# Seven block products in place of eight for the gate and up products of two FFNs

## The chip, the cores and the metric

The kernel runs on one core of a Trainium2 chip. The metric is the device time of one execution, in microseconds (us); lower is better. The engines run side by side, each through its own queue in order: TensorE (PE in the profile, its weight loads PEld), VectorE (DVE), ScalarE (ACT), GpSimd (POOL) and SyncE (SP), which here issues the loads of the weights. An instruction that waits for another engine's result holds up everything behind it in its own queue.

## The reference

A decoder trunk of two layers on x of 512 tokens by 1024 features, float32. Each layer is half an FFN, a token mixer, half an FFN; a last norm follows.

```python
def rmsnorm(x, g):
    xf = x.astype(jnp.float32)
    r = lax.rsqrt(jnp.mean(xf * xf, axis=-1, keepdims=True) + EPS)
    return (xf * r * g.astype(jnp.float32)).astype(x.dtype)

def swiglu(h, w_gate, w_up, w_down):
    return (jax.nn.silu(h @ w_gate) * (h @ w_up)) @ w_down

def reference(x, ...):
    for layer in range(DEPTH):
        x = x + 0.5 * swiglu(rmsnorm(x, ffn1_norm[layer]), ...)
        h = rmsnorm(x, mix_norm[layer])
        x = x + (parallel_s5_stickbreak(h, ...) if layer % 2 == 0 else short_conv_mixer(h, ...))
        x = x + 0.5 * swiglu(rmsnorm(x, ffn2_norm[layer]), ...)
    return rmsnorm(x, final_norm)
```

The hidden width of an FFN is 2752: 21 blocks of 128 and a tail of 64. There are four FFNs, numbered 0 to 3 in the order in which they run: FFN 0, mixer, FFN 1, FFN 2, short convolution, FFN 3. The change touches FFN 1 and FFN 2.

## The kernel before, in words

x lies transposed in SBUF, features on partitions: eight tiles of 128 features by 512 tokens. A product of float32 numbers is made of three passes of a shorter format (float32r): each operand is cut into a high part (a cast to that format, on ScalarE) and a low part (the rest, a subtraction on VectorE), and TensorE adds high times high, low times high and high times low in PSUM (`mm3`, L245 to L247). So one weight unit of 128 by 1024 is loaded to `raw` by SP (L196), cast to `whi` by ScalarE (L207), subtracted to `wlo` by VectorE (L213), and used by 8 x 3 = 24 matmuls with 512 columns (tokens). There are three buffers each of `raw`, `whi` and `wlo`. A unit is cut two units ahead of its use (`advance`, AHEAD = 2), and the load three units further is issued then.

An FFN goes by thirds of the hidden blocks. In a third, each block f has a gate unit and an up unit (a pair); the products go to PSUM banks `ps_A` (six buffers). VectorE multiplies the gate bank by the norm's factor `rb` (L421), ScalarE takes silu (L423), VectorE multiplies again by `rb` (L424) and by the up bank (L433), ScalarE casts the result to `hhi` (L434) and VectorE makes `hlo` (L435). The tail of gate and up is one unit of both. Then eight down units (one for each block of x) multiply with these, into `ps_mm` (two buffers), and VectorE adds half of it to x (L479). In the last third of an FFN the next norm's inputs are made from x there.

The order on every engine is that of the program text, since this part is under a manual schedule: `drive` walks a list of steps, and a unit's step is `advance` (the cut of a later unit), the unit's own products, and its evacuation (`after`). The mixer in between is ordered by a planner of its own that the change does not touch. The last down stage of the kernel (L533 to L545) works on halves of 256 tokens: it is the only place where the kernel before runs long rows of matmuls with 256 columns.

Of the kernel before, what the change touches and what calls it, by code (L numbers as in the profile page):

```python
# [18 lines left out]
S = 512  # L19
NK = D // 128  # L20
EPS = 1e-6
THIRDS = [list(range(0, 8)), list(range(8, 15)), list(range(15, 22))]
TAIL = 21
RAW_BUFS = 3
W_BUFS = 3
AHEAD = 2
# [21 lines left out]
class Unit:  # L48


    def __init__(self, src, cols, products, after):
        self.src, self.cols, self.products, self.after = src, cols, products, after
        self.own = None


class Task:
# [83 lines left out]
class Trunk:  # L140
# [52 lines left out]
    def load(self, n):  # L193
        u = self.units[n]
        u.raw = self.wp.tile([128, 1024], F32, tag="raw", name="raw", bufs=RAW_BUFS)
        self.nc.sync.dma_start(u.raw[:, : u.cols], u.src)  # L196
        self.loaded = n + 1

    def split_tile(self, u, tag):
# [9 lines left out]
    def cut_lo(self, n, engine=None):  # L209
# [6 lines left out]
    def advance(self):  # L216

        n = self.split
        if n < len(self.units):
            self.cut_hi(n)  # L220
            self.cut_lo(n)
        if n + RAW_BUFS < len(self.units):
            self.load(n + RAW_BUFS)

    def drive(self):

        self.prologue()
        for s in self.steps:
            if isinstance(s, Unit):
                if s.own is None:  # L230
# [171 lines left out]
    def ffn(self, n, nxt):  # L402

        st = self
        gu, dn = self.a["gu"], self.a["dn"]
        first = [True]
        nc = self.nc

        def begin():
            st.take_xg()  # L410
            st.h = {}

        self.steps.append(begin)
# [24 lines left out]

        def evac_tail(keep):
            def run():  # L440
                pg = keep[0]
                t = st.fp.tile([128, S], F32, tag="t", name="t", bufs=2)
                s = st.fp.tile([128, S], F32, tag="s", name="s", bufs=2)
                nc.vector.tensor_tensor(t[0:64], pg[0:64], st.rb[0:64], ALU.mult)
                nc.scalar.activation(s[64:128], t[0:64], AF.Silu)
                nc.vector.tensor_tensor(s[64:128], s[64:128], st.rb[64:128], ALU.mult)
                nc.vector.tensor_tensor(s[64:128], pg[64:128], s[64:128], ALU.mult)
                both = st.fp.tile([128, S], F32R, tag="hhi", name="both", bufs=8)
                hi = st.fp.tile([128, S], F32R, tag="hlo", name="hi2", bufs=8)
                nc.scalar.copy(hi[64:128], s[64:128])  # L450
                nc.scalar.copy(both[0:64], s[64:128])
                nc.vector.tensor_tensor(both[64:128], s[64:128], hi[64:128].bitcast(F32), ALU.subtract)
                nc.scalar.copy(hi[0:64], s[64:128])
                nc.gpsimd.memset(hi[64:128].bitcast(F32), 0.0)
                st.h[TAIL] = (both, hi)
            return run

        def down(dt, third):
            fs = THIRDS[third]
# [23 lines left out]
            c0 = sum(len(THIRDS[i]) for i in range(third)) * 128  # L483
            return Unit(dn[n, dt, :, c0:c0 + nf * 128], nf * 128, products, after)

        for third in range(3):
            for f in sorted(THIRDS[third], key=lambda f: (f != TAIL, f)):
                keep = []
                if f == TAIL:
                    st.steps.append(Unit(gu[n, 2 * f], 1024, st.over_x("A", keep), evac_tail(keep)))  # L490
                    continue
                g, u = evac_gate(keep, f), evac_up(keep, f)
                if f == 0:
                    early, keep0 = [g, u], keep
# [12 lines left out]
                pair = [Unit(gu[n, 2 * f], 1024, st.over_x("A", keep), g), Unit(gu[n, 2 * f + 1], 1024, st.over_x("A", keep), u)]
                if f == 0 and n == st.first_ffn:
                    pair[0].products = lambda u, p=pair, k=keep: st.over_x_two("A", p, [k, k])
                    pair[1].products = lambda u: None  # L510
                st.steps += pair
            if third == 2 and nxt == 6:
                st.steps.insert(-1, st.advance)
                st.steps.append(st.advance)
                st.last_down([down(dt, third) for dt in range(NK)])
                break
            for dt in range(NK):
                st.steps.append(down(dt, third))

    def last_down(self, units):  # L520

# [2 lines left out]

        st, nc = self, self.nc
        v = nc.vector
        fs = THIRDS[2]
# [456 lines left out]
    def mixer(self, nxt):  # L984
# [538 lines left out]
        def run():  # L1523
# [6 lines left out]
            for n in range(st.split, end + AHEAD):  # L1530
# [15 lines left out]
    def prologue(self):  # L1546
# [192 lines left out]
```

## Time and profile before

| | |
|---|---|
| median of 3 runs | 1861.44 us (1861.14 to 1862.04) |
| the profiled execution's own time | 1861.36 us |
| its span, first to last instruction | 1859.6 us |
| matmuls on TensorE | 8486 |
| mean granted clock of TensorE | 0.995 |
| VectorE busy | 1044.9 us |
| ScalarE busy | 627.6 us |

Matmuls are pipelined: a 512-column matmul shows 0.39 us in the profile, and the next begins 0.227 us after it began. So a stretch of matmuls is timed from start to start. The other engines' durations are those of one instruction, and the next may begin slightly before its end. Where an engine stood idle, a row says for how long and which instruction released it.

### The profile page before, as it was taken

Reading aid. Unit: us, or ns where it says so; the run is one execution under the profiler, and the core shown is the slowest. Engines: PE = TensorE matmul, PEld = TensorE weight load, DVE = VectorE, ACT = ScalarE, POOL = GpSimd, SP = SyncE. Lnnn points to the kernel's source line nnn. Section 1 sums busy time; section 2 is a strip of 40 time slices with the busy share of each in tenths; the row PEclk is TensorE's granted clock in tenths of the full one; section 3 lists DMA queues with packets and bytes.
Section 4 is the critical chain, followed back from the end, with each engine's and each line's share of the span. In section 5 each row is a group of like instructions: output and inputs, shape, how many; then the busy total and the mean of one; then the engine's idle time right before and its main releaser. Section 6 shows DMA issues by size and latency. Waiting matters only on the chain.

```text
span 1859.6 us, 21763 instructions
## 1 busy us (share of the span) xinstructions
PE 1837.4 (99%) x8486; PEld 1527.0 (82%) x8486; DVE 1044.9 (56%) x1609; ACT 627.6 (34%) x893; POOL 115.6 (6%) x238
## 2 busy tenths in 40 slices
PE   9999999999989999999999999999999999999998
PEld 8887888888867888888888888888888888888888
DVE  6657778656887553444455434445655554344454
ACT  5313222434885332222243222233322333222233
POOL 0280000100000100000010000000100100000000
PEclk9999999999989999999999999999999999999999
DMA  4334344446411233233332323333322223323231
GB/s 163 116 97 148 113 143 135 136 163 220 125 46 58 83 109 102 91 91 102 95 109 91 102 91 94 99 102 89 105 100 93 91 91 102 102 92 98 97 102 66
DMA packets 77829, 197.71 MB, mean 106 GB/s; under 512 B 20304, under 2 KB 27488, under 8 KB 77728
## 3 DMA queue, kind: packets, MB, share of 16 engines
q1 hardware_dynamic: 77552, 196.30, 33.1%
q8 instruction: 66, 1.08, 0.2%
q14 instruction: 35, 0.29, 0.0%
q10 hardware_dynamic: 144, 0.03, 0.0%
q0 software_dynamic: 32, 0.01, 0.0%
HBM read 180.45 MB, written 12.58 MB: 104 GB/s over the span
## 4 chain that ended last, share of the span: by engine, by line
PE 90%; POOL 3%; DVE 3%; ACT 2%; issue 1%; DMA 1%; DVEq 0%; SPq 0%; POOLq 0%; ACTq 0%
PE ps_A L245 19%; PE ps_A L247 19%; PE ps_A L246 19%; PE ps_mm L245 8%; PE ps_mm L247 8%; PE ps_mm L246 8%; PE ps_mm L1442 1%; PE ps_A L1037 1%; PE ps_A L1039 1%; PE ps_A L1038 1%; PE ps_mm L1443 1%; PE ps_mm L1444 1%; PE ps_mm L1037 0%; DVE wlo L213 0%; PE ps_mm L1038 0%
## 5 line engine op out<-in xcount | busy, mean ns | idle before, releaser
L245 PE MATMUL ps_A<-xhi,whi 128*128 128x512 f32 x1568 | 611.6, 390 | 0.4 <-ACT xhi L297 0.4
L246 PE MATMUL ps_A<-xhi,wlo 128*128 128x512 f32 x1568 | 610.4, 389 | 1.4 <-DVE wlo L213 1.4
L247 PE MATMUL ps_A<-xlo,whi 128*128 128x512 f32 x1568 | 610.3, 389 | 0.1
L213 DVE TENSOR_TENSOR wlo<-raw,whi 128x1024 fp32r<-128x1024 f32 (+1 forms) x324 | 398.7, 1231 | 137.2 <-ACT whi L207 135.9
L207 ACT CAST whi<-raw 128x1024 fp32r<-128x1024 f32 (+1 forms) x324 | 331.9, 1025 | 386.3 <-PE ps_mm L247 228.3
L246 PEld LDWEIGHTS ps_A<-xhi,wlo 128*128 128x128 f32 x1568 | 294.4, 188 | 63.4 <-DVE wlo L213 2.3
L245 PEld LDWEIGHTS ps_A<-xhi,whi 128*128 128x128 f32 x1568 | 294.4, 188 | 62.0 <-issue 0.8
L247 PEld LDWEIGHTS ps_A<-xlo,whi 128*128 128x128 f32 x1568 | 294.3, 188 | 61.8 <-DVE xlo L303 0.5
L245 PE MATMUL ps_mm<-hhi,whi 128*128 128x512 f32 (+1 forms) x672 | 256.6, 382 | 0.0
L246 PE MATMUL ps_mm<-hhi,wlo 128*128 128x512 f32 (+1 forms) x672 | 256.3, 381 | 0.0
L247 PE MATMUL ps_mm<-hlo,whi 128*128 128x512 f32 (+1 forms) x672 | 256.3, 381 | 0.0
L423 ACT ACTIVATE s<-t 128x512 f32<-128x512 f32 x84 | 53.1, 632 | 290.3 <-DVE t L421 290.3
L479 DVE SCALAR_TENSOR_TENSOR x<-ps_mm,x 128x512 f32<-128x512 f32 x88 | 60.8, 691 | 155.8 <-PE ps_mm L247 148.4
L434 ACT CAST hhi<-s 128x512 fp32r<-128x512 f32 x84 | 52.2, 621 | 284.9 <-DVE s L433 284.9
L245 PEld LDWEIGHTS ps_mm<-hhi,whi 128*128 128x128 f32 x672 | 126.3, 188 | 24.5 <-issue 0.4
L247 PEld LDWEIGHTS ps_mm<-hlo,whi 128*128 128x128 f32 x672 | 126.3, 188 | 24.4
L246 PEld LDWEIGHTS ps_mm<-hhi,wlo 128*128 128x128 f32 x672 | 126.3, 188 | 24.3
L421 DVE TENSOR_TENSOR t<-ps_A,rb 128x512 f32<-128x512 f32 x84 | 57.9, 690 | 108.4 <-PE ps_A L247 102.3
L433 DVE TENSOR_TENSOR s<-ps_A,s 128x512 f32<-128x512 f32 x84 | 58.0, 690 | 104.1 <-PE ps_A L247 103.4
L424 DVE TENSOR_TENSOR s<-s,rb 128x512 f32<-128x512 f32 x84 | 58.2, 692 | 63.3 <-ACT s L423 63.3
L435 DVE TENSOR_TENSOR hlo<-s,hhi 128x512 fp32r<-128x512 f32 x84 | 58.2, 693 | 57.7 <-ACT hhi L434 57.7
L297 ACT ACTIVATE xhi<-x,norms 128x512 fp32r<-128x512 f32 x48 | 34.5, 723 | 99.1 <-DVE x L479 60.8
(348 smaller groups left out, 1574.3 us busy)
## 6 DMA issues: line engine op xcount, KB each, us to landing
raw<-gu SPq DMA_DIRECT2D x170, 512.0 KB, 3.3
raw<-dn SPq DMA_DIRECT2D x64, 448.0 KB, 3.3
raw<-dn SPq DMA_DIRECT2D x32, 512.0 KB, 3.5
raw<-sci SPq DMA_DIRECT2D x24, 512.0 KB, 3.3
raw<-ab SPq DMA_DIRECT2D x16, 512.0 KB, 3.3
raw<-abo SPq DMA_DIRECT2D x8, 512.0 KB, 3.3
raw<-sco SPq DMA_DIRECT2D x8, 512.0 KB, 3.3
x<-xT SPq DMA_DIRECT2D x8, 256.0 KB, 5.4
```

What stands on the lines that cost most here:

```text
L207: self.nc.scalar.copy(u.hi[:, : u.cols], u.raw[:, : u.cols])
L213: (engine or self.nc.vector).tensor_tensor(u.lo[:, :c], u.raw[:, :c], u.hi[:, :c].bitcast(F32), ALU.subtract)
L245: nc.tensor.matmul(ps, whi, xhi, start=start and i == 0, stop=False)
L246: nc.tensor.matmul(ps, wlo, xhi, start=False, stop=False)
L247: nc.tensor.matmul(ps, whi, xlo, start=False, stop=stop and i == n - 1)
L421: nc.vector.tensor_tensor(t, pg, st.rb, ALU.mult)
L423: nc.scalar.activation(s, t, AF.Silu)
L424: nc.vector.tensor_tensor(s, s, st.rb, ALU.mult)
L433: nc.vector.tensor_tensor(s, pu, s, ALU.mult)
L434: nc.scalar.copy(hi, s)
L435: nc.vector.tensor_tensor(lo, s, hi.bitcast(F32), ALU.subtract)
L479: nc.vector.scalar_tensor_tensor(x, keep[0], 0.5, x, ALU.mult, ALU.add)
```

## The change

In FFN 1 and FFN 2 the blocks are dealt out anew: the tail goes to the first third (after block 1), and the second and last thirds hold seven full blocks each, so 14 pairs per FFN, 28 in all. For these, gate and up of one block are taken as one 256 by 1024 matrix in two by two parts (gate or up, first or second half of the features), and normalized x as two by two parts (first or second half of the features, first or second half of the tokens). The four parts of the result come from seven block products with sums of the parts in place of eight products of parts. Each of the seven has four k-blocks of 128 and three passes, with 256 columns. The sums of weights (`s12`, `s34`) are made from `raw` on VectorE for every pair and cut to high and low like weights (`shi`, `slo`; the up unit's second half becomes `ahi`, `alo`). x is normalized with `rb` first (`seven_x`), then its sums are made once per FFN, beside the first third's down units (`seven_sums`, `seven_lower`). The results are recombined by adds on VectorE between the products, two of them from banks into which a later product accumulates.

```diff
+PLAIN_THIRDS = [list(range(0, 8)), list(range(8, 15)), list(range(15, 22))]
+SEVEN_THIRDS = [list(range(0, 7)) + [TAIL], list(range(7, 14)), list(range(14, 21))]
+SEVEN = (1, 2)
+THIRDS = [SEVEN_THIRDS if n in SEVEN else PLAIN_THIRDS for n in range(4)]
...
+    def cuts(self, count):
+
+        for _ in range(count):
+            n = self.split
+            if n < len(self.units):
+                if self.units[n].mate is not None:
+                    yield from self.cut_mate(n)
+                    continue
+                self.cut_hi(n)
+                self.cut_lo(n)
+                if self.units[n].paired:
+                    yield
+                    continue
+            self.refill(n)
+            yield
+
+    def cut_mate(self, n):
...
+        nc.scalar.copy(u.q_hi, w[:, b])
+        v.tensor_tensor(s[0][:, a], w[:, a], w[:, b], ALU.add)
+        yield
+        v.tensor_tensor(s[0][:, b], s[0][:, a], g[:, a], ALU.subtract)
+        nc.scalar.copy(u.s_hi[0], s[0])
+        yield
+        v.tensor_tensor(s[1][:, a], g[:, a], w[:, a], ALU.subtract)
+        v.tensor_tensor(s[1][:, b], g[:, b], s[0][:, b], ALU.subtract)
+        nc.scalar.copy(u.s_hi[1], s[1])
+        yield
+        v.tensor_tensor(u.q_lo, w[:, b], u.q_hi.bitcast(F32), ALU.subtract)
+        self.split = n + 1
+        self.refill(n - 1)
+        self.refill(n)
+        yield
+        for i in range(2):
+            v.tensor_tensor(u.s_lo[i], s[i], u.s_hi[i].bitcast(F32), ALU.subtract)
+            yield
...
         for third in range(3):
-            for f in sorted(THIRDS[third], key=lambda f: (f != TAIL, f)):
+            seven = n in SEVEN and third
+            if seven:
+                pairs = [(Unit(gu[n, 2 * f], 1024, None, None), Unit(gu[n, 2 * f + 1], 1024, None, None)) for f in thirds[third]]
+                for f, (g, u) in zip(thirds[third], pairs):
+                    g.paired, u.mate = True, g
+                    st.steps += [[g, u], lambda f=f, u=u: st.seven_products(f, u)]
+                st.steps.append(st.flush)
...
             for dt in range(NK):
-                st.steps.append(down(dt, third))
+                s = down(dt, third)
+                more = n in SEVEN and third < 2
+                if more and dt == 6:
+                    st.steps.append(st.advance)
+                s.split_before = more and dt == 7
+                st.steps.append(s)
+                if more and third == 0:
+                    st.steps += [lambda p=p: p() for p in st.seven_parts(dt)]
...
+    def seven_products(self, f, u):
...
+        cut = self.cuts(2)
+        more = lambda: next(cut, None)
...
+        def product(ps, w, c, b, first):
+
+            for k in range(4):
+                hi, lo = (p[:, c + k * 128:c + k * 128 + 128] for p in w)
+                xhi, xlo = b(k)
+                for n, (a, m) in enumerate(((hi, xhi), (lo, xhi), (hi, xlo))):
+                    nc.tensor.matmul(
+                        ps, a, m, start=first and k == 0 and n == 0, stop=k == 3 and n == 2, skip_group_check=True)
...
+        product(x, gate, 0, b11, True)
+        more()
+        nc.scalar.copy(p1, x)
+        self.flush()
+        y = self.bank("A")[:, l]
+        product(y, s12, 512, t2, True)
+        more()
+        v.tensor_tensor(u1, y, p1, ALU.add)
+        product(x, gate, 512, b21, False)
+        more()
+        nc.scalar.activation(s[:, l], x, AF.Silu)
+        more()
+        product(y, s12, 0, t1, False)
+        more()
+        v.tensor_tensor(u3, y, p1, ALU.add)
+        z = self.bank("A")[:, l]
+        product(z, s34, 0, t3, True)
+        more()
+        v.tensor_tensor(up[:, r], z, u3, ALU.add)
+        product(y, s34, 512, b22, False)
+        more()
+        v.tensor_tensor(s[:, r], y, p1, ALU.add)
+        nc.scalar.activation(s[:, r], s[:, r], AF.Silu)
+        product(z, (u.q_hi, u.q_lo), 0, t4, False)
+        v.tensor_tensor(up[:, l], z, u1, ALU.add)
+        v.tensor_tensor(s, s, up, ALU.mult)
+        hi = self.fp.tile([128, S], F32R, tag="hhi", name="hhi", bufs=8)
+        lo = self.fp.tile([128, S], F32R, tag="hlo", name="hlo", bufs=8)
+        nc.scalar.copy(hi, s)
+        self.h[f] = (hi, lo)
+        self.pending = lambda: v.tensor_tensor(lo, s, hi.bitcast(F32), ALU.subtract)
+        deque(cut, maxlen=0)
```

What this does to the queues is seen in the middle of FFN 1's second third. On VectorE before, one pair of units stands like this (`t` and `s` are the evacuation of the gate, `wlo` the cuts):

```order
L421 TENSOR_TENSOR t<-ps_A,rb 128x512
L424 TENSOR_TENSOR s<-s,rb 128x512
L213 TENSOR_TENSOR wlo<-raw,whi 128x1024
L433 TENSOR_TENSOR s<-ps_A,s 128x512
L435 TENSOR_TENSOR hlo<-s,hhi 128x512
L213 TENSOR_TENSOR wlo<-raw,whi 128x1024
```

And in the changed program, on VectorE, from the last adds of one pair into the next pair (`u` is u1, `alo` the low part of the up unit's second half):

```order
L706 TENSOR_TENSOR s<-ps_A,up 128x256
L709 TENSOR_TENSOR up<-ps_A,u_6857 128x256
L710 TENSOR_TENSOR s<-s,up 128x512
L220 TENSOR_TENSOR wlo<-raw,whi 128x1024
L715 TENSOR_TENSOR hlo<-s,hhi 128x512
L263 TENSOR_TENSOR s_7021<-raw 128x512
L692 TENSOR_TENSOR u_6986<-ps_A,up 128x256
L265 TENSOR_TENSOR s_7021<-s_7021,raw 128x512
L268 TENSOR_TENSOR s_7022<-raw 128x512
L269 TENSOR_TENSOR s_7022<-raw,s_7021 128x512
L272 TENSOR_TENSOR alo<-raw,ahi 128x512
L699 TENSOR_TENSOR s<-ps_A,up 128x256
```

The cut of a later gate unit now stands between the multiply of one pair (L710) and the first add of the next (L692), with `hlo` and a weight sum behind it.

On ScalarE before, in the same place (`s` is silu):

```order
L423 ACTIVATE s<-t 128x512
L207 CAST whi<-raw 128x1024
L434 CAST hhi<-s 128x512
L207 CAST whi<-raw 128x1024
L423 ACTIVATE s<-t 128x512
```

And in the changed program on ScalarE, from the second silu of one pair into the next (`up` is the copy of the first product):

```order
L707 ACTIVATE s<-s 128x256
L713 CAST hhi<-s 128x512
L214 CAST whi<-raw 128x1024
L687 COPY up<-ps_A 128x256
L262 CAST ahi<-raw 128x512
L266 CAST shi<-s_7279 128x1024
L695 ACTIVATE s<-ps_A 128x256
L270 CAST shi<-s_7280 128x1024
```

The gate unit's cast stands behind the cast of the finished pair (L713) as before, and the copy of the next pair's first product (L687) stands behind it.

## Rows read from the trace of the kernel before

**Rows 1.** The page: busy time, and the chain of waits, by engine.

```profile
PE 1837.4 (99%) x8486; PEld 1527.0 (82%) x8486; DVE 1044.9 (56%) x1609; ACT 627.6 (34%) x893; POOL 115.6 (6%) x238
...
PE 90%; POOL 3%; DVE 3%; ACT 2%; issue 1%; DMA 1%; DVEq 0%; SPq 0%; POOLq 0%; ACTq 0%
```

**Rows 2.** FFN 1 by stretch: busy PE, PEld, DVE, ACT, POOL; clock, DMA.

```profile
698.50:742.00 43.50, 43.50 (x193) 36.02 (x193) 16.02 (x17) 8.96 (x9) 0.00 (x0) 1.00 0.33 101
...
742.00:818.00 76.00, 76.00 (x337) 62.92 (x336) 35.57 (x41) 21.31 (x27) 0.00 (x0) 1.00 0.29 92
```

**Rows 3.** Matmuls in order of time (start, duration, engine, line).

```profile
1772.64 0.39 PE L245 MATMUL ps_A<-xhi,whi 128*128 128x512 f32 x1
...
1775.36 0.39 PE L245 MATMUL ps_A<-xhi,whi 128*128 128x512 f32 x1
...
1812.83 0.28 PE L245 MATMUL ps_A<-hhi,whi 128*128 128x256 f32 x1
...
1814.27 0.28 PE L245 MATMUL ps_A<-hhi,whi 128*128 128x256 f32 x1
```

**Rows 4.** Weight loads by line and shape: busy, mean ns.

```profile
L246 PEld LDWEIGHTS ps_A<-hhi,wlo 128*128 128x128 f32 x48 | 9.2, 192 | 0.0
```

**Rows 5.** A hand-over from TensorE to VectorE, in order of time.

```profile
1835.20 0.28 PE L545 MATMUL ps_mm<-hi,wlo 128*128 128x256 f32 x1
...
1835.52 0.42 DVE L550 SCALAR_TENSOR_TENSOR x<-ps_mm,x 128x256 f32<-128x256 f32 x1 [0.57 <-PE ps_mm L545]
```

**Rows 6.** VectorE operations by line and shape: busy, mean ns, idle before.

```profile
L435 DVE TENSOR_TENSOR hlo<-s,hhi 128x512 fp32r<-128x512 f32 x84 | 58.2, 693 | 57.7 <-ACT hhi L434 57.7
...
L550 DVE SCALAR_TENSOR_TENSOR x<-ps_mm,x 128x256 f32<-128x256 f32 x8 | 3.4, 424 | 4.3 <-PE ps_mm L545 4.3
```

**Rows 7.** VectorE and ScalarE in order of time; a pair in FFN 1.

```profile
776.05 0.69 DVE L433 TENSOR_TENSOR s<-ps_A,s 128x512 f32<-128x512 f32 x1 [1.82 <-PE ps_A L247]
...
776.78 0.62 ACT L434 CAST hhi<-s 128x512 fp32r<-128x512 f32 x1 [3.80 <-DVE s L433]
...
777.30 1.05 ACT L207 CAST whi<-raw 128x1024 fp32r<-128x1024 f32 x1
...
778.38 1.23 DVE L213 TENSOR_TENSOR wlo<-raw,whi 128x1024 fp32r<-128x1024 f32 x1 [0.26 <-ACT whi L207]
```

**Rows 8.** VectorE operations that follow one another, in order of time.

```profile
331.99 0.69 DVE L424 TENSOR_TENSOR s<-s,rb 128x512 f32<-128x512 f32 x1 [0.76 <-ACT s L423]
...
332.60 0.68 DVE L928 TENSOR_TENSOR qt<-qsi 128x512 f32<-128x512 f32 x1
...
399.57 1.22 DVE L213 TENSOR_TENSOR wlo<-raw,whi 128x1024 fp32r<-128x1024 f32 x1 [0.81 <-ACT whi L207]
...
400.71 0.68 DVE L1226 SCALAR_TENSOR_TENSOR qk<-ps_A,rb 128x512 f32<-128x512 f32 x1
...
1222.01 1.23 DVE L213 TENSOR_TENSOR wlo<-raw,whi 128x1024 fp32r<-128x1024 f32 x1 [1.55 <-ACT whi L207]
...
1223.26 0.69 DVE L421 TENSOR_TENSOR t<-ps_A,rb 128x512 f32<-128x512 f32 x1
...
1288.94 1.09 DVE L213 TENSOR_TENSOR wlo<-raw,whi 128x896 fp32r<-128x896 f32 x1 [0.60 <-ACT whi L207]
```

**Rows 9.** The page: loads of gate and up, KB, us to landing.

```profile
raw<-gu SPq DMA_DIRECT2D x170, 512.0 KB, 3.3
```

**Rows 10.** TensorE's gaps in the mixer, and its granted clock by stretch.

```profile
520.55 0.33 PE L1373 MATMUL ps_mm<-wh,v 128*128 128x128 f32 x1 [1.79 <-ACT sig L1467]
...
535.68 0.33 PE L1340 MATMUL ps_A<-sph,mk_neg 128*128 128x128 f32 x1 [1.11 <-DVE sp L1314]
...
538.90 0.47 PE L1340 MATMUL ps_A<-sph,mk_tri 128*128 128x128 f32 x1 [1.46 <-DVE sp L1314]
...
521.00:528.00 7.00, 6.03 (x18) 0.51 0.19 69
...
539.00:540.00 1.00, 1.00 (x5) 0.50 0.00 0
```

More of the change, by code (lines that the diff above doesn't have):

```diff
@@ L52, in __init__ @@
         self.src, self.cols, self.products, self.after = src, cols, products, after
-        self.own = None
+        self.own = self.mate = None
+        self.paired = self.split_before = False
 class Task:
@@ L195, in load @@
         u.raw = self.wp.tile([128, 1024], F32, tag="raw", name="raw", bufs=RAW_BUFS)
-        self.nc.sync.dma_start(u.raw[:, : u.cols], u.src)
+        at = 0
+        for src in u.src if isinstance(u.src, list) else [u.src]:
+            self.nc.sync.dma_start(u.raw[:, at:at + src.shape[-1]], src)
+            at += src.shape[-1]
         self.loaded = n + 1
@@ L214, in cut_lo, with refill, advance @@
         self.split = n + 1
[L216 to L221, printed above, removed]
+    def refill(self, n):
         if n + RAW_BUFS < len(self.units):
             self.load(n + RAW_BUFS)
+    def advance(self):
+        deque(self.cuts(1), maxlen=0)
+    def cuts(self, count):
[13 more added lines that the diff above has]
+    def cut_mate(self, n):
+        nc, sp = self.nc, self.sp7
+        v = nc.vector
+        u = self.units[n]
+        g, w = u.mate.raw, u.raw
+        a, b = slice(0, 512), slice(512, 1024)
+        u.q_hi = sp.tile([128, 512], F32R, tag="ahi", name="ahi", bufs=2)
+        u.q_lo = sp.tile([128, 512], F32R, tag="alo", name="alo", bufs=2)
+        s = [sp.tile([128, 1024], F32, tag="s12", name="s12"), sp.tile([128, 1024], F32, tag="s34", name="s34")]
+        u.s_hi = [sp.tile([128, 1024], F32R, tag="shi", name="shi", bufs=3) for _ in range(2)]
+        u.s_lo = [sp.tile([128, 1024], F32R, tag="slo", name="slo", bufs=3) for _ in range(2)]
+        nc.scalar.copy(u.q_hi, w[:, b])
[16 more added lines that the diff above has]
+            yield
     def drive(self):
@@ L229, in drive @@
             if isinstance(s, Unit):
-                if s.own is None:
+                if s.own is None and not s.split_before:
                     self.advance()
@@ L407, in ffn @@
         nc = self.nc
+        thirds = THIRDS[n]
         def begin():
@@ L411, in begin @@
             st.h = {}
+            if n == SEVEN[0]:
+                st.open("sp7")
         self.steps.append(begin)
@@ L458, in down @@
         def down(dt, third):
-            fs = THIRDS[third]
+            fs = thirds[third]
             nf = len(fs)
@@ L481, in after @@
                     st.feed_norm(nxt, dt)
-            c0 = sum(len(THIRDS[i]) for i in range(third)) * 128
-            return Unit(dn[n, dt, :, c0:c0 + nf * 128], nf * 128, products, after)
+            src = [dn[n, dt, :, fs[0] * 128:(fs[-1] + 1) * 128]]
+            if fs[-1] - fs[0] != nf - 1:
+                src = [dn[n, dt, :, fs[0] * 128:(fs[-2] + 1) * 128], dn[n, dt, :, TAIL * 128:(TAIL + 1) * 128]]
+            return Unit(src, nf * 128, products, after)
         for third in range(3):
-            for f in sorted(THIRDS[third], key=lambda f: (f != TAIL, f)):
+            seven = n in SEVEN and third
[5 more added lines that the diff above has]
+                st.steps.append(st.flush)
+            for f in [] if seven else sorted(thirds[third], key=lambda f: (f != TAIL or third == 0, f if f != TAIL else 1.5)):
                 keep = []
@@ L511, in ffn @@
                 st.steps += pair
+                if n in SEVEN and 3 <= f < 7:
+                    st.steps.append(lambda i=f - 3: st.seven_x(n, i))
             if third == 2 and nxt == 6:
@@ L517, in ffn @@
             for dt in range(NK):
-                st.steps.append(down(dt, third))
+                s = down(dt, third)
[6 more added lines that the diff above has]
+                    st.steps += [lambda p=p: p() for p in st.seven_parts(dt)]
+        if n == SEVEN[-1]:
+            st.steps.append(lambda: st.open_pools.pop().__exit__(None, None, None))
@@ new lines, in seven_x @@
+    def seven_x(self, n, i):
+        tag = ("s12", "s34", "slo", "slo")[i]
+        if i == 0:
+            self.xn, self.b7, self.t7, self.pending = {}, {}, {}, None
+        self.xn[i] = self.sp7.tile([128, 1024], F32, tag=tag, name="xn", bufs=3 if tag == "slo" else 1)
+        for j in range(2):
+            k = i + 4 * j
+            self.nc.vector.scalar_tensor_tensor(
+                self.xn[i][:, j * 512:(j + 1) * 512], self.x[k], self.norms[:, (0, 2, 3, 5)[n], k:k + 1], self.rb, ALU.mult, ALU.mult)
@@ new lines, in seven_parts, with seven_sums @@
+    def seven_parts(self, dt):
+        i = {0: 0, 1: 1, 3: 2, 5: 3}.get(dt)
+        j = {1: 0, 2: 1, 4: 2, 6: 3}.get(dt)
+        return [lambda: self.seven_sums(i)] * (i is not None) + [lambda: self.seven_lower(j)] * (j is not None)
+    def seven_sums(self, i):
+        nc, v, x = self.nc, self.nc.vector, self.xn[i]
+        b11, b12, b21, b22 = (x[:, c:c + 256] for c in range(0, 1024, 256))
+        t = self.fp.tile([128, 512], F32, tag="t", name="t12", bufs=2), self.fp.tile([128, 512], F32, tag="s", name="t34", bufs=2)
+        l, r = slice(0, 256), slice(256, 512)
+        hi = [self.xgp.tile([128, 512], F32R, tag="xhi", name="thi") for _ in range(2)]
+        b = self.sp7.tile([128, 768], F32R, tag="bhi", name="bhi", bufs=4)
+        v.tensor_tensor(t[0][:, l], b12, b11, ALU.subtract)
+        nc.scalar.copy(b[:, 0:256], b11)
+        v.tensor_tensor(t[0][:, r], b22, t[0][:, l], ALU.subtract)
+        nc.scalar.copy(hi[0], t[0])
+        v.tensor_tensor(t[1][:, l], b22, b12, ALU.subtract)
+        v.tensor_tensor(t[1][:, r], b21, t[0][:, r], ALU.subtract)
+        nc.scalar.copy(hi[1], t[1])
+        nc.scalar.copy(b[:, 256:768], x[:, 512:1024])
+        self.t7[i], self.b7[i] = [t, hi], [b]
@@ new lines, in seven_lower @@
+    def seven_lower(self, i):
+        v, x = self.nc.vector, self.xn[i]
+        t, hi = self.t7[i]
+        lo = [self.xgp.tile([128, 512], F32R, tag="xlo", name="tlo") for _ in range(2)]
+        for a, h, o in zip(t, hi, lo):
+            v.tensor_tensor(o, a, h.bitcast(F32), ALU.subtract)
+        b = self.b7[i][0]
+        o = self.sp7.tile([128, 768], F32R, tag="blo", name="blo", bufs=4)
+        v.tensor_tensor(o[:, 0:256], x[:, 0:256], b[:, 0:256].bitcast(F32), ALU.subtract)
+        v.tensor_tensor(o[:, 256:768], x[:, 512:1024], b[:, 256:768].bitcast(F32), ALU.subtract)
+        self.t7[i], self.b7[i] = (hi, lo), (b, o)
@@ new lines, in flush, with part, total @@
+    def flush(self):
+        if self.pending is not None:
+            self.pending()
+        self.pending = None
+    def seven_products(self, f, u):
+        nc, v, g = self.nc, self.nc.vector, u.mate
+        cut = self.cuts(2)
+        more = lambda: next(cut, None)
+        l, r = slice(0, 256), slice(256, 512)
+        def product(ps, w, c, b, first):
[5 more added lines that the diff above has]
+                        ps, a, m, start=first and k == 0 and n == 0, stop=k == 3 and n == 2, skip_group_check=True)
+        def part(j):
+            return lambda k: [p[:, j * 256:j * 256 + 256] for p in self.b7[k]]
+        def total(j):
+            c = slice(j % 2 * 256, j % 2 * 256 + 256)
+            return lambda k: [p[j // 2][:, c] for p in self.t7[k]]
+        b11, b21, b22 = (part(j) for j in range(3))
+        t1, t2, t3, t4 = (total(j) for j in range(4))
+        gate, s12, s34 = (g.hi, g.lo), (u.s_hi[0], u.s_lo[0]), (u.s_hi[1], u.s_lo[1])
+        s = self.fp.tile([128, S], F32, tag="s", name="s", bufs=2)
+        up = self.fp.tile([128, S], F32, tag="t", name="up", bufs=2)
+        p1, u3 = up[:, l], s[:, r]
+        u1 = self.tp.tile([128, S], F32, tag="sq", name="u1", bufs=2)[:, l]
+        x = self.bank("A")[:, l]
+        product(x, gate, 0, b11, True)
[30 more added lines that the diff above has]
+        deque(cut, maxlen=0)
@@ L526, in last_down @@
         v = nc.vector
-        fs = THIRDS[2]
+        fs = THIRDS[3][2]
         out = st.a["out"]
```

1 line of the change is left out of this document (removed).

## The prediction

> **What bounds the kernel now.** I began with the page's busy line and the engine shares of its chain of waits [rows 1]: TensorE is busy 99% of the 1859.6 us span and is 90% of the chain. Next came the busy time by stretch, inside the stretches that the change rewrites [rows 2]. In the second FFN's (FFN 1's) second third, 742 to 818 us, TensorE is busy 76.00 of 76.00 us at granted clock 1.00, VectorE 35.57, ScalarE 21.31. Nothing but the matmul stream sets the time there, so I priced that stream: twelve 512-column matmuls take 1775.36 - 1772.64 = 2.72 us [rows 3], 0.2267 each. A gate and up pair is 2 x 8 x 3 = 48 of them: 10.88 us.
>
> **The change: TensorE's own work.** Seven products of 4 k-blocks x 3 passes are 84 matmuls of 256 columns. The last down stage runs such matmuls, each with its own weights: twelve take 1814.27 - 1812.83 = 1.44 us [rows 3], 0.120 each. The weight loads are busy 192 ns each [rows 4] yet set no pace there. So a pair needs 84 x 0.120 = 10.08 us, 0.80 less; for 28 pairs 22.4 us. Halving the columns saves less than half of a matmul (0.120 against 0.113), so an eighth less arithmetic is 7% less time.
>
> **A page against the row.** The Trainium skill ("TensorE: Matmul & The Clock Gate", Back-to-back issue gap) gives N/2.4 + 2.5 ns per matmul. By it, as an estimate, the pair would fall from 10.36 to 9.17 us and the loop below would be 11.06 against 10.36, slower again by 0.7. The rows above are longer at both sizes; the sum goes by them.
>
> **What the change adds beside TensorE: a loop.** Call the products P1 to P7 in their order in seven_products. P1's result is copied (ScalarE, L687), then P3 accumulates into its bank; P2's bank is read by u1 (L692), then P4 accumulates into it. So P4 may not start until u1 is done; likewise P6 waits for u3 and P7 for the add at L703. Now VectorE is strictly in order, and u1 stands behind: the previous pair's last add (L709, after P7), its multiply (L710), the next pair's wlo (L220), hlo of the previous pair, one weight sum (L263). And wlo waits for whi, which on ScalarE stands behind hhi (L713), which waits for that multiply. This is a ring that closes once per pair: P4, P5, P6, P7, add, multiply, hhi, whi, wlo, hlo, sum, u1, P4. Queued behind the held wlo is all other VectorE work of the pair, and TensorE's queue stops at P4.
>
> Its price, from rows:
> - P4 to P7: 48 x 0.120 = 5.76 us.
> - The end of P7: the last matmul lasts 0.28, 0.16 beyond its place in the stream, and VectorE starts 0.04 later [rows 5]: 0.20.
> - Add at 256 columns from PSUM: 0.42 [rows 6]; 0.03 to the next.
> - Multiply, hhi, whi, up to the start of wlo: the kernel before runs exactly this chain, from the multiply at 776.05 to wlo at 778.38 [rows 7]: 2.33 us (0.69, 0.62 of which whi overlaps the last 0.10, 1.05, hand-overs).
> - wlo, hlo, sum: instructions that need not wait start 0.08 before their predecessor ends. 331.99 to 332.60 is 0.61 for a 0.69 us operation, 399.57 to 400.71 is 1.14 for 1.22 [rows 8]. So 1.15 + 0.61 + 0.61 = 2.37.
> - u1 0.42, and 0.05 to TensorE, an estimate from the hand-overs in rows 5 and 7 (0.03 to 0.04).
>
> From the end of P7 in the stream to P4 that is 0.20 + 0.45 + 2.33 + 2.37 + 0.47 = 5.82 us. TensorE has only P1 to P3 for it, 36 x 0.120 = 4.32: it stands 1.50 us per pair, 0.4 of it ahead of P3 (the copy of P1 stands behind whi) and 1.1 ahead of P4. Period: 5.76 + 5.82 = 11.58 us, against 10.88 before. The kernel before has the same chain with no harm: a cut there is made two units (10.9 us) ahead of its use, and no accumulation waits for VectorE in mid-product.
>
> Is VectorE itself the limit? Its fifteen instructions per pair, back to back, are 3 x 1.15 + 7 x 0.61 + 5 x 0.34 = 9.4 us, plus 1.65 idle while hhi and whi run: 11.1. Close, but the ring is longer.
>
> **Sum over the stretches.** Each of four stretches has seven pairs. The first finds its cuts done in the down units and P4 not late: 10.08 us in the two last thirds. In the two second thirds the eighth down unit has no room: VectorE must in two units of 23 x 0.2267 = 5.21 us do x (0.69), four sums (1.5), wait for ScalarE's casts until 4.6, then wlo, five 512-wide and two 1024-wide operations (6.5), x and the last tlo and blo (2.2): its blo comes some 13.4 us after the start, P1's last block wants it at 11.7. I take 1.7 plus 0.3 at P4: 12.1. In each last pair the sum before u1 is replaced by a second wlo of 896 columns (1.09 against 0.69 [rows 8, 6]) and both wlo are that size: 11.86. The other twenty are 11.58. Total 2 x 10.08 + 2 x 12.1 + 4 x 11.86 + 20 x 11.58 = 323.4, against 28 x 10.88 = 304.6: 18.8 us slower.
>
> **What costs nothing.** The tail block moves from the last third to the first: the same 24 matmuls, and its short down product (two instead of three) goes along. The eight normalizing operations (8 x 0.69 [rows 6]) lie in the first third, the x sums and their parts (some 4.2 us of VectorE for each of four) beside the downs, where VectorE is busy 16.02 of 43.50 us [rows 2]; the last of them is charged above, and without that cover each would cost its length. The 16 extra 64 KB loads of down weights stand on SP's queue, two units before use. Loads of a pair now go out as two in a row after the cut; at 3.3 us to landing each [rows 9], even end to end they have landed 6.6 us after issue, 2 us ahead of the next cut. If that margin fails, whi waits and the ring grows by as much. TensorE's own sequence of banks needs three of six per pair, so none is short.
>
> The profiled run's own time is 1861.36 us (span 1859.6), the median of the runs shown 1861.44; so I add to 1861.4: **1880 us**, 1% slower.
>
> **Rivals.**
> 1. *Instructions on VectorE do not overlap.* With waits on nearly every one of them, each could start after its predecessor's end: 1222.01 to 1223.26 is 1.25 for 1.23 [rows 8]. Then VectorE itself is the limit: 3 x 1.23 + 7 x 0.69 + 5 x 0.42 + 1.75 + 0.2 = 12.5 us per pair, and with the longer first pairs 42 us in all: 1903. Against it, the two other pairs in that group: wlo there had waits too, long met. By a rule of the Trainium skill ("VectorE: DVE Perf Modes", The DRAIN you can't avoid) the next operation starts only when the pipeline is empty, except for one that isn't held; the trace agrees with the exception, mostly. 0.14.
> 2. *The clock falls in the gaps.* In the mixer TensorE stood 1.79 us before 520.55, and the granted clock in 521 to 528 was 0.51, the 1.2 GHz level, for 7 us [rows 10]. My gaps are 1.1 and 0.4 per pair, smaller singly but recurrent, and 1.7 at two places. Seven us at half speed lose 3.5 us of matmul time; a fall within P4 to P7 costs about 3 of them, since that half of the ring is TensorE's own. Three to ten falls: 1889 to 1910; in every pair, 1955. In the mixer again, a gap of 1.11 us before 535.68 left the clock up, and a second of 1.46 before 538.90 brought it to 0.50 in 539 to 540 [rows 10]: two such gaps within 4.3 us are more than mine. 0.19.
> 3. *The ring is hidden, TensorE stays the bound: faster.* This holds if the path from P7 to u1 takes at most 4.32 us; below 5.12 the change breaks even (5.76 + 5.12 = 10.88). Then the time is 1861.4 - 22.4 + 4 for the starts of the second thirds = 1843. For it: TensorE has no wait at all in these stretches today, and VectorE is less than half busy [rows 2]. Against it: 2.33 us of the path is measured as one piece, and nothing in the order of the two queues lets whi pass hhi. 0.08.
> 4. *About no change*, the ring near 10.9 because some of wlo, hlo and the sum is shorter than in these rows: 0.05.
>
> Were the weight loads to set the pace after all (192 ns each), a pair would take 16.1 us and the kernel 146 us more; rows 3 and 4 exclude it.
>
> **How the numbers follow.** My case has 0.54 and its own range is 1872 to 1889 (0.3 us per ring either way). The time is its 1880. The range for 8 in 10 leaves out the faster rival and the clock falling in every pair: 1864 to 1912. A measurement here tells 0.2%, 3.7 us, from no change. Faster: 0.08; same: 0.05; slower: 0.87.
>
> **What would show it.** Right: in the seven-product stretches TensorE waits some 0.4 us before P3 (for L687) and 1.1 us before P4 (for L692), VectorE's longest wait there is wlo for whi, some 1.65 us per pair, and P1 of successive pairs are 11.6 us apart; outside these stretches nothing moves. Matmuls of 256 columns come every 0.120 us. Wrong: no waits of TensorE there and a pair of 10.1 us; or a granted clock under 1.00 in them (rival 2); or VectorE with no idle time and pairs of 12.5 us (rival 1).

## The result, and the profile after

The changed kernel takes 1884.41 us (median of four, 1882.82 to 1886.18) beside 1861.29 us for the kernel before in the same session (median of four): ratio 1.0126, 95% interval 1.0108 to 1.0143. It is slower by 1.3%; 1880 was forecast, inside 1864 to 1912. The profiled execution took 1882.82 us, with a span of 1881.1.

The page of the changed kernel, busy time and the chain by engine, answers to [rows 1]:

```profile
PE 1828.1 (97%) x9494; PEld 1558.1 (83%) x9494; DVE 1204.3 (64%) x1941; ACT 697.9 (37%) x1037; POOL 115.5 (6%) x238
...
PE 80%; DVE 8%; ACT 5%; issue 3%; POOL 3%; DMA 0%; DVEq 0%; SPq 0%; POOLq 0%; ACTq 0%
```

TensorE is busy 9.3 us less than before, so the time did not go into matmuls. Its share of the chain fell from 90% to 80%, and VectorE (3% to 8%) and ScalarE (2% to 5%) took most of what it lost. The stretches of FFN 1 (busy PE, PEld, DVE, ACT, POOL; clock; DMA) say where, in answer to [rows 2]:

```profile
746.00:817.00 71.00, 63.95 (x511) 61.52 (x509) 53.40 (x85) 29.23 (x47) 0.00 (x0) 1.00 0.25 87
865.00:935.00 70.00, 62.95 (x501) 60.52 (x501) 53.17 (x84) 28.46 (x46) 0.00 (x0) 1.00 0.26 86
700.00:734.00 34.00, 34.00 (x152) 28.15 (x151) 25.59 (x43) 16.79 (x25) 0.00 (x0) 1.00 0.29 87
```

In both seven-product stretches TensorE stands idle 7 us of 70, where it had no gap in 76 [rows 2]; in the downs (700 to 734) it still has none. The clock is 1.00 throughout. What it waits for stands in the view of its waits (us in total, times, longest):

```profile
PE ps_A L667 <- DVE u L692: 21.3, 24, 1.1
PE ps_A L667 <- ACT up L687: 6.9, 24, 0.3
...
PE ps_A L302 <- DVE wlo L220: 2.9, 3, 1.4
PE ps_A L667 <- DVE blo L645: 2.9, 2, 1.4
```

Twenty-four of 28 pairs wait for u1 (L692) and for the copy of P1 (L687); the other four are the first of each stretch, whose cuts were made in the downs. The last two rows are smaller waits, below. VectorE's own waits, for the five pairs between 746 and 805 us:

```profile
DVE wlo L220 <- ACT whi L214: 8.2, 5, 1.6
DVE up L709 <- PE ps_A L667: 2.2, 5, 0.4
```

VectorE stands 1.64 us per pair ahead of wlo. One turn of the ring in order of time, from the end of P7 to the next P4:

```profile
781.52 0.28 PE L667 MATMUL ps_A<-tlo,ahi 128*128 128x256 f32 x1
...
781.84 0.42 DVE L709 TENSOR_TENSOR up<-ps_A,u 128x256 f32<-128x256 f32 x1 [0.44 <-PE ps_A L667]
...
782.37 0.69 DVE L710 TENSOR_TENSOR s<-s,up 128x512 f32<-128x512 f32 x1
...
783.09 0.62 ACT L713 CAST hhi<-s 128x512 fp32r<-128x512 f32 x1 [1.25 <-DVE s L710]
...
783.62 1.04 ACT L214 CAST whi<-raw 128x1024 fp32r<-128x1024 f32 x1
...
784.57 0.36 ACT L687 COPY up<-ps_A 128x256 f32<-128x256 f32 x1
784.69 1.22 DVE L220 TENSOR_TENSOR wlo<-raw,whi 128x1024 fp32r<-128x1024 f32 x1 [1.63 <-ACT whi L214]
...
784.98 0.38 PE L667 MATMUL ps_A<-bhi,whi 128*128 128x256 f32 x1 [0.31 <-ACT up L687]
...
785.84 0.68 DVE L715 TENSOR_TENSOR hlo<-s,hhi 128x512 fp32r<-128x512 f32 x1
...
786.44 0.68 DVE L263 TENSOR_TENSOR s<-raw 128x512 f32<-128x512 f32 x1
787.04 0.41 DVE L692 TENSOR_TENSOR u<-ps_A,up 128x256 f32<-128x256 f32 x1
...
787.51 0.39 PE L667 MATMUL ps_A<-thi,shi 128*128 128x256 f32 x1 [0.84 <-DVE u L692]
```

Each line starts when the one that it waits for, for its operand or in its queue, is done: the add, the multiply, hhi, whi, then wlo, with u1 three instructions behind it, and P4 behind u1. TensorE's two rows with a bracket are its two stops of the turn (0.31 before P3, 0.84 before P4). They come to less than the 1.65 us by which the pair is longer than 10.08: a matmul's modelled end (0.28) reaches 0.16 past its place in the stream, and the first matmul after a stop lasts 0.38 to 0.39, 0.1 more. So a stop costs its row and about 0.25. This 0.25 counts as busy in the record; 50 such stops are some 12.5 us, an estimate, and so TensorE's busy time fell by 9.3 us and not by the 22.4 of its shorter work.

From the first matmul of each pair to the next, the pairs of FFN 1's second third take 12.03 us, then 11.73 for the five in the middle, then 11.89; those of its last third 10.07, 11.73 for the five and 11.89; and FFN 2 the same. The 28 pairs take 326.4 us against 304.6.

### The profile page after: what moved, and what is told of

The parts are those of the page before. It is cut to its first block, busy times and chain, and to the rows that moved or that the text cites. A ratio compares the mean times of both kernels' runs of the same rounds, so it can differ in the third digit from the quotient of the medians.

```text
span 1881.1 us, 24317 instructions
## 1 busy us (share of the span) xinstructions
PE 1828.1 (97%) x9494; PEld 1558.1 (83%) x9494; DVE 1204.3 (64%) x1941; ACT 697.9 (37%) x1037; POOL 115.5 (6%) x238
## 4 chain that ended last, share of the span: by engine, by line
PE 80%; DVE 8%; ACT 5%; issue 3%; POOL 3%; DMA 0%; DVEq 0%; SPq 0%; POOLq 0%; ACTq 0%
PE ps_A L302 13%; PE ps_A L301 13%; PE ps_A L303 13%; PE ps_A L667 10%; PE ps_mm L301 7%; PE ps_mm L302 7%; PE ps_mm L303 7%; ACT whi L214 2%; DVE wlo L220 1%; DVE s L710 1%; DVE hlo L715 1%; ACT hhi L713 1%; DVE s L263 1%; PE ps_mm L1640 1%; PE ps_A L1235 1%
## 5 line engine op out<-in xcount | busy, mean ns | idle before, releaser
L302 PE MATMUL ps_A<-xhi,wlo 128*128 128x512 f32 x1120 | 436.4, 390 | 3.0 <-DVE wlo L220 2.9
L301 PE MATMUL ps_A<-xhi,whi 128*128 128x512 f32 x1120 | 437.6, 391 | 0.1
L303 PE MATMUL ps_A<-xlo,whi 128*128 128x512 f32 x1120 | 436.0, 389 | 0.1
L302 PEld LDWEIGHTS ps_A<-xhi,wlo 128*128 128x128 f32 x1120 | 210.3, 188 | 47.8 <-DVE wlo L220 4.4
L301 PEld LDWEIGHTS ps_A<-xhi,whi 128*128 128x128 f32 x1120 | 210.2, 188 | 45.4 <-ACT whi L214 0.9
L303 PEld LDWEIGHTS ps_A<-xlo,whi 128*128 128x128 f32 x1120 | 210.2, 188 | 44.3 <-DVE xlo L359 0.5
L301 PEld LDWEIGHTS ps_mm<-hhi,whi 128*128 128x128 f32 x672 | 126.3, 188 | 24.6 <-issue 0.4
L667 PE MATMUL ps_A<-thi,shi 128*128 128x256 f32 x336 | 97.7, 291 | 21.3 <-DVE u L692 21.3
L667 PE MATMUL ps_A<-thi,slo 128*128 128x256 f32 x336 | 95.0, 283 | 0.0
L667 PE MATMUL ps_A<-tlo,shi 128*128 128x256 f32 x336 | 95.0, 283 | 0.0
L667 PEld LDWEIGHTS ps_A<-thi,shi 128*128 128x128 f32 x336 | 64.3, 191 | 26.6 <-DVE u L692 26.6
```

The source lines that it names most:

```text
L301: nc.tensor.matmul(ps, whi, xhi, start=start and i == 0, stop=False)
L302: nc.tensor.matmul(ps, wlo, xhi, start=False, stop=False)
L303: nc.tensor.matmul(ps, whi, xlo, start=False, stop=stop and i == n - 1)
L667: nc.tensor.matmul(ps, a, m, start=first and k == 0 and n == 0, stop=k == 3 and n == 2, skip_group_check=True)
```

## The experiments

All are edits of the changed kernel; times are medians, ratios stand against the kernel before on the same chip.

**The gate unit's whi ahead of hhi.** The ring has hhi before whi only because the next gate unit is cut after the pair is finished. Here its high part is cast behind P7 and ahead of the add; a few further lines, not shown, keep it from being cast a second time and leave the last pair of a third as it is.

```diff
         product(z, (u.q_hi, u.q_lo), 0, t4, False)
+        deque(cut, maxlen=0)
+        if not last:
+            self.cut_hi(self.split)
+            self.units[self.split].early = True
         v.tensor_tensor(up[:, l], z, u1, ALU.add)
...
-        deque(cut, maxlen=0)
```

> One edit of the changed kernel: on ScalarE the cast of the next gate unit's weights (whi) stands ahead of the finished pair's cast hhi instead of behind it; VectorE's order and its work are the same. Theory (the ring through multiply, hhi, whi, wlo, u1): VectorE no longer stands 1.65 us per pair ahead of wlo, the path from P7 to u1 falls from 5.9 to 4.3 us, as long as P1 to P3, TensorE's waits before P3 and P4 go, a pair is 10.1 us (10.08 by matmuls) and the time 1842 to 1848 us, faster than the kernel before. Rival (VectorE's total work per pair is the limit): a pair stays above 11 us and the time above 1865 us.

Measured: 1846.86 us (1845.44 to 1847.52), ratio 0.9924 [0.9908, 0.9941]; the middle pairs take 10.08 us, the last of each third 10.56. A stretch of it (busy PE, PEld, DVE, ACT, POOL; clock):

```profile
749.00:800.00 51.00, 51.00 (x427) 51.00 (x426) 47.82 (x77) 26.07 (x41) 0.00 (x0) 1.00 0.29 101
```

VectorE and ScalarE there, in order of time (L715 is the multiply, L718 hhi):

```profile
768.86 1.03 ACT L214 CAST whi<-raw 128x1024 fp32r<-128x1024 f32 x1
769.54 0.69 DVE L715 TENSOR_TENSOR s<-s,up 128x512 f32<-128x512 f32 x1
770.15 1.22 DVE L220 TENSOR_TENSOR wlo<-raw,whi 128x1024 fp32r<-128x1024 f32 x1
770.27 0.62 ACT L718 CAST hhi<-s 128x512 fp32r<-128x512 f32 x1 [0.38 <-DVE s L715]
```

TensorE has no gap, with the same instructions as the changed kernel and the same order on VectorE, and wlo follows the multiply after 0.61 us in place of 2.32. So 37.5 us hang on the order of two casts on ScalarE. VectorE's work in full (47.82 of 51.00 us) fits under the products.

**Two subtractions on VectorE left out**, those of the weight sums' low parts; the high parts stand in for them.

```diff
-        u.s_lo = [sp.tile([128, 1024], F32R, tag="slo", name="slo", bufs=3) for _ in range(2)]
+        u.s_lo = u.s_hi
...
-            v.tensor_tensor(u.s_lo[i], s[i], u.s_hi[i].bitcast(F32), ALU.subtract)
```

> One edit of the changed kernel: the two 1024-wide subtractions per pair that make the low parts of the weight sums are left out (the high parts are used in their place, so these two low passes compute something else); 2.3 us less of VectorE per pair, none of it on the path from P7 to u1. Theory (ring): no change, 1881 to 1887 us, TensorE's waits for u1 and for the copy as before. Rival (VectorE's total work is the limit): the pair falls towards TensorE's 10.08 us and the time to 1842 to 1852 us.

Measured: 1880.90 us (1879.82 to 1883.21), ratio 1.0110 [1.0095, 1.0125]. The middle pairs stay at 11.73, and TensorE's waits are those of the changed kernel:

```profile
PE ps_A L666 <- DVE u L691: 21.3, 24, 1.1
PE ps_A L666 <- ACT up L686: 6.9, 24, 0.3
```

VectorE is busy 1145.8 us by the page in place of 1204.3, 2.1 us less per pair, and no turn of the ring got shorter: VectorE's load is not what bounds the pair. The medians are 3.5 us apart, about the spread of these four runs (3.4). In the traces the pairs differ in the first of each second third alone, 10.07 in place of 12.03, where these operations stood ahead of blo: 3.9 us for the two.

**u1 ahead of wlo.** The copy of P1 and u1 are issued before the cut, and hlo after it.

```diff
         product(x, gate, 0, b11, True)
-        more()
         nc.scalar.copy(p1, x)
-        self.flush()
...
         v.tensor_tensor(u1, y, p1, ALU.add)
+        more()
+        self.flush()
+        more()
```

> One edit of the changed kernel: u1 is issued on VectorE ahead of wlo, hlo and the first weight sum of the pair, and the copy of P1 ahead of whi on ScalarE. Theory (an in-order VectorE that is held for 1.65 us per pair, and then meets the next bank into which TensorE accumulates): the wait before P4 goes and comes back at P6, which waits for u3 behind the same work: some 1.6 us per pair there, pair 11.7 us, time 1881 to 1890 us. Rival (u1's place alone is at fault): the waits go, pair 10.1 us, time 1842 to 1848 us.

Measured: 1883.14 us (1882.49 to 1884.03), ratio 1.0120 [1.0105, 1.0136]; the middle pairs take 11.84. Beside the late blo of two first pairs, TensorE's waits in the pairs are down to one:

```profile
PE ps_A L667 <- DVE s L699: 33.0, 24, 1.5
```

The stops at P3 and P4 are gone, and one of 1.48 us stands at P6 of each middle pair, for u3 (L699), longer than the two together (1.15). In order of time:

```profile
786.74 0.42 DVE L689 TENSOR_TENSOR u<-ps_A,up 128x256 f32<-128x256 f32 x1 [1.73 <-PE ps_A L667]
...
787.09 1.22 DVE L220 TENSOR_TENSOR wlo<-raw,whi 128x1024 fp32r<-128x1024 f32 x1
...
792.43 0.39 PE L667 MATMUL ps_A<-bhi,shi 128*128 128x256 f32 x1 [1.48 <-DVE s L699]
```

The place of the wait is the expected one, but not what holds VectorE: wlo does not stand for whi any more. VectorE stands 1.73 us ahead of u1, which waits for P2, and wlo follows u1 without a gap (whi, done at 786.89, would have held it nearly as long). So this order closes another ring, 11.84 us long: P6, P7, the next P1 and P2, u1, then wlo, hlo, the four weight sums, alo and u3 on VectorE, and P6 again.

**hlo alone behind u1.**

```diff
-        self.flush()
...
         v.tensor_tensor(u1, y, p1, ALU.add)
+        self.flush()
```

> One edit of the changed kernel: hlo of the finished pair stands on VectorE behind u1 instead of ahead of it; the same fifteen instructions per pair. Theory (ring): it is shorter by one 512-wide operation, 0.60 us, in the 24 pairs that are not the first of a stretch: 14 us less, 1870 us (1867 to 1873), pairs of 11.13 us. Rival (VectorE's total work is the limit): no change, 1881 to 1887 us.

Measured: 1880.92 us (1878.61 to 1883.13), ratio 1.0108 [1.0093, 1.0123]; pairs 11.61, not 11.13. This missed. TensorE's waits:

```profile
PE ps_A L667 <- DVE u L691: 7.3, 24, 0.6
PE ps_A L667 <- ACT up L687: 6.9, 24, 0.3
PE ps_A L667 <- DVE s L699: 4.1, 20, 0.2
```

The wait for u1 fell to a third, but one for u3 came, 0.2 us in each of 20 pairs. In order of time:

```profile
755.89 0.42 DVE L691 TENSOR_TENSOR u<-ps_A,up 128x256 f32<-128x256 f32 x1
756.22 0.68 DVE L715 TENSOR_TENSOR hlo<-s,hhi 128x512 fp32r<-128x512 f32 x1
...
759.23 0.42 DVE L699 TENSOR_TENSOR s<-ps_A,up 128x256 f32<-128x256 f32 x1
...
759.70 0.39 PE L667 MATMUL ps_A<-bhi,shi 128*128 128x256 f32 x1 [0.20 <-DVE s L699]
```

hlo is behind u1 now but still ahead of u3, and P6 waits for u3. There is a second ring, from P6 and P7 over the add, multiply, hhi, whi, wlo and all of VectorE's queue up to u3. The move does not shorten it; it is 11.61 us long here, 0.12 less than the first ring was, and that 0.12 is what a middle pair gained. The last pair of each third has no weight sums ahead of u3 and no wait for it, and there the same move gained 0.49 (11.40 in place of 11.89), near the 0.60 expected.

**Two moves, and the low parts left out.** If several rings of nearly one length is the reason, hlo behind u1, alo behind u3 and the two subtractions out shorten all of them.

```diff
-            v.tensor_tensor(u.s_lo[i], s[i], u.s_hi[i].bitcast(F32), ALU.subtract)
...
-        self.flush()
...
         v.tensor_tensor(u1, y, p1, ALU.add)
+        self.flush()
...
-        more()
         v.tensor_tensor(u3, y, p1, ALU.add)
+        more()
```

> The kernel without the two slo subtractions (as e2, the high parts stand for them), with hlo behind u1 and alo behind u3 on VectorE. In e7 moving hlo alone brought 0.12 us a pair in place of 0.60. Theory (several rings through the one VectorE queue: the move lengthened the ring over u3 to 11.61 us, and one over the add at L703 is as long): with alo and slo out of these too, the ring over u1 is the longest again, 11.13 us a pair, 14 us below e2: 1866.5 us (1864 to 1870). Rival (the moved hlo costs something else, whatever the rings): still within 3 us of e2's 1880.9.

Measured: 1866.50 us (ten runs, 1863.64 to 1869.85), ratio 1.0027 [1.0018, 1.0037]; pairs 11.12.

```profile
PE ps_A L666 <- DVE u L690: 7.2, 24, 0.6
PE ps_A L666 <- ACT up L686: 6.9, 24, 0.3
```

The wait for u3 is gone, the one for u1 is as in the run before, and the middle pair has the 11.1 us that the first ring alone gives with hlo out of it. The missed expectation had the ring right and had overlooked its neighbours. What the move of alo and the two subtractions each gave beyond that is not separated by this run.

**The x sums earlier**, so that the last blo is done before the second third begins.

```diff
-        i = {0: 0, 1: 1, 3: 2, 5: 3}.get(dt)
-        j = {1: 0, 2: 1, 4: 2, 6: 3}.get(dt)
+        i = {0: 0, 1: 1, 2: 2, 4: 3}.get(dt)
+        j = {1: 0, 2: 1, 3: 2, 5: 3}.get(dt)
```

> One edit of the changed kernel: the third and the fourth sum of x and their low parts are made one down unit earlier, so that the last of them leaves VectorE before the cut of the first pair begins. Theory (the first pair of each second third waits for blo behind that cut): its wait at the end of P1 (1.44 us in the trace, twice) goes, that pair takes 10.1 us in place of 12.03, 3.9 us less in all: 1880.5 us (1878 to 1883). Rival (VectorE is over its share in those down units whichever way they are dealt out): a wait of the same size moves into the down units or stays, 1884 us.

Measured: 1880.17 us (1879.82 to 1881.11), ratio 1.0094 [1.0079, 1.0110]. The first pair takes 10.07 in place of 12.03, no wait for blo is left, and the ring is as it was:

```profile
PE ps_A L667 <- DVE u L692: 21.2, 24, 1.1
```

**Seven products in FFN 2 alone.**

```diff
-SEVEN = (1, 2)
+SEVEN = (2,)
```

> The changed kernel with the seven products in FFN 2 alone; FFN 1 as in the kernel before. Theory (each stretch pays by itself): half of the 23 us, 1872.8 us (1870 to 1875); the stretches of FFN 2 as in the changed kernel (11.73 us a pair) and FFN 1 at 10.88. Rival (a part of the loss is shared, as the pool that stays open across both FFNs or the handover between them): not half, below 1868 or above 1877 us.

Measured: 1872.58 us (1872.51 to 1874.38), ratio 1.0056 [1.0038, 1.0074], half of the loss with half of the pairs and half of the waits:

```profile
PE ps_A L667 <- DVE u L692: 10.6, 12, 1.1
PE ps_A L667 <- ACT up L687: 3.5, 12, 0.3
```

**Three edits together**: whi ahead of hhi, the x sums earlier, and the tail unit one block later in the first third.

```diff
-            for f in [] if seven else sorted(thirds[third], key=lambda f: (f != TAIL or third == 0, f if f != TAIL else 1.5)):
+            for f in [] if seven else sorted(thirds[third], key=lambda f: (f != TAIL or third == 0, f if f != TAIL else 2.5)):
```

> Three edits of the changed kernel: whi ahead of hhi, the x sums one down unit earlier, and the tail unit of FFN 1 and FFN 2 after block 2 in place of block 1. Theory: the first is worth 37.5 us as measured alone, the second 3.9, the third takes the two waits for wlo behind the tail's evacuation (0.77 us each and a restart, 1.9 in all): 1841 us (1839 to 1844), 1.1% faster than the kernel before. Rival (with whi out of the way VectorE has no room left, so the sums or the tail push their waits elsewhere): 1845 to 1848 us.

Measured: 1839.23 us (1837.53 to 1839.96), ratio 0.9873 [0.9857, 0.9888]: 21.8 us under the kernel before and the fastest of all here. Pairs are 10.07, five of 10.08, and 10.56.

```profile
PE ps_A L303 <- DVE wlo L220: 1.4, 1, 1.4
...
PE ps_A L668 <- DVE u L693: 0.9, 4, 0.2
```

What is left of the waits is the one for wlo that the kernel before had too (1.4 us, once) and 0.2 in each last pair. Of the 22.4 us that the arithmetic saves, 20.5 arrive in the 28 pairs; the rest is the four last pairs of 10.56.

## Why the prediction was right, point by point

**TensorE's own work: right.** Pairs that do not wait take 10.07 to 10.08 us, as the cadence in [rows 3] gave. By the Trainium skill ("TensorE: Matmul & The Clock Gate", Back-to-back issue gap) such a pair was to take 9.17 us and the ring 11.06, as an estimate from its formula; the trace disagrees at both, with 10.07 and 11.73.

**The ring: right in every link, 0.15 us too short.** Link by link, from the rows of one turn:

| Link | forecast | measured |
|---|---|---|
| P4 to the add after P7 | 5.96 | 6.06 |
| add to multiply | 0.45 | 0.53 |
| multiply to wlo | 2.33 | 2.32 |
| wlo to u1 | 2.37 | 2.35 |
| u1 to P4 | 0.47 | 0.47 |
| period | 11.58 | 11.73 |

The first link lacked the longer first matmul after a stop (0.10), the second the gap before an operation that needs its predecessor's result: the multiply starts 0.11 after the add's end, where 0.03 was taken. Less the 0.03 by which the next two links were shorter, that is 0.15 a pair and 3.0 us over 20 pairs, the first term of the sum that was mis-sized. That it is these links that close, and not VectorE's load, is what the experiments show: the first opens it at one link and all 1.65 us of the middle pairs go, the second takes load away and their length stays.

By the Trainium skill ("TensorE: Matmul & The Clock Gate", Architectural detail) the queues of ScalarE and VectorE are strictly first in, first out; the trace agrees: u1's operands lay ready and it started 0.08 before the end of the last instruction ahead of it, at 787.04.

**First and last pairs: right, the last by some luck.** 12.03 for 12.1 and 11.89 for 11.86. The last pair was put 0.28 above the middle ones and lies 0.16 above: the sum had left out that its whi is shorter too (0.94 us in place of 1.04), and the ring's 0.15 made up for that. The first was put down to a late blo and that holds: the matmul that wants blo stands 1.44 us. Around it are rows for the tail (order of time, the changed kernel):

```profile
646.28 0.62 ACT L513 CAST hi<-s 64x512 fp32r<-64x512 f32 x1
...
646.92 1.05 ACT L214 CAST whi<-raw 128x1024 fp32r<-128x1024 f32 x1
...
648.00 1.22 DVE L220 TENSOR_TENSOR wlo<-raw,whi 128x1024 fp32r<-128x1024 f32 x1 [1.55 <-ACT whi L214]
...
649.28 0.50 PE L302 MATMUL ps_A<-xhi,wlo 128*128 128x512 f32 x1 [0.77 <-DVE wlo L220]
...
736.85 0.42 DVE L645 TENSOR_TENSOR blo<-xn,bhi 128x256 fp32r<-128x256 f32 x1
...
737.33 0.39 PE L667 MATMUL ps_A<-blo,whi 128*128 128x256 f32 x1 [1.44 <-DVE blo L645]
...
1014.63 0.50 PE L302 MATMUL ps_A<-xhi,wlo 128*128 128x512 f32 x1 [0.76 <-DVE wlo L220]
```

**"What costs nothing": wrong for the tail.** The first four and the last of those rows are in the first thirds, right behind the tail unit's place. There whi stands behind the tail's own casts on ScalarE (L513 the last of them), wlo behind whi, and TensorE waits. The prediction moved the same 24 matmuls and took the move to cost nothing. The last 264 matmuls of gate and up in the first third take 61.61 us in FFN 1 and 61.05 in FFN 2, and 61.60 and 61.05 with the x sums earlier; with the tail one block later as well (the last experiment) they take 60.14 and 59.84, and both waits are gone. That is 1.5 and 1.2 us, 2.7 in both FFNs, more than the two rows of 0.77 and 0.76. The kernel before has no such wait in its first thirds. The x sums cost no more than the late blo that was charged for them: the downs of FFN 1's first third, beside which they stand, take 41.71 us for 184 matmuls, 0.2267 each, and 43.52 for 192, the same pace, in the kernel before. The extra loads and the loads in twos cost nothing, as said: no engine waits for a load in the seven-product stretches.

**The sum.** Pairs +21.8 (18.8 forecast) and tails +2.7 (nothing forecast) make 24.5. From the first matmul of FFN 1 to that of FFN 2, and through FFN 2, the traces differ by 12.4 and 12.2, 24.6 in all. The profiled executions differ by only 21.5, because the part ahead of FFN 1, whose code is the same, was 3.0 us shorter in this one; the medians differ by 23.1.

**The rivals.** VectorE that does not overlap (12.5 us a pair; its terms add to 12.57): its instructions start 0.60 apart at 0.68 each in the ring, it idles 1.64 us a pair, and less work on it gained nothing there. One reason given against this rival was misread: in [rows 8] wlo at 399.57 had itself just stood 0.81 us for whi, so its wait was not long met; what those rows show is that the instruction behind it started early. A falling clock: 1.00 in both stretches. A hidden ring: not in this order; it needs the path from P7 to u1 to be at most 4.32 us. The first experiment brings it to 4.15 by taking hhi and whi out of it (0.20 to the add, 3.48 from there to u1, 0.47 to P4), and then the time is 1846.86, close to the 1843 of that rival. No change: no link was much shorter than its row.

## What to carry to other kernels

Where a product accumulates into a bank that another engine reads in between, that product, and every one behind it, waits on that engine's queue: follow the queue back from the read, and if it leads, here over a third engine, to the previous block's last product, there is a ring. The longest ring, where it is longer than each engine's own work, sets the time per block. Look for the instruction in it that has no business there (here a cast of weights that stood behind a cast of results) and issue it earlier; that was worth 37.5 us, where less work on VectorE by itself was worth nothing in the ring. Before moving only one instruction, measure the next longest ring: here it was 0.12 us away.

## What the runs showed of the hardware that was not expected

- The first matmul of 256 columns after a stop takes 0.38 to 0.39 us in the record, others 0.28, and the next starts 0.22 to 0.23 later in place of 0.12; with 512 columns it takes 0.50 at 649.28, others 0.39. So a stop costs about 0.1 us more than the delay of its first matmul.
- A VectorE operation on its predecessor's result started 0.11 us after that one's end from add to multiply, and 0.03 after it from the first weight sum to the second with u1 ahead of wlo (788.82 and 789.54), while an independent one starts 0.08 before it. What makes it 0.11 or 0.03 stays open.
- Stops of TensorE of 0.31 and 0.84 us, every 11.7 us, left the granted clock at 1.00 in both stretches, and so did one of 1.48 us every 11.84 us (u1 ahead of wlo, 760 to 817 us and 865 to 935). In the mixer a single one of 1.79 was followed by 0.51, and one of 1.46, with one of 1.11 shortly before it, by 0.50 [rows 10]. So the length of a stop does not tell by itself whether the clock falls.
